# Seven products in another order, their token forms read beside the last gates, and the combined weights made beside linear attention

## The chip, the cores and the metric

The kernel runs on one core of one Trainium2 chip. The core has engines that run their own instruction queues in parallel: TensorE (PE, matmuls, with its weight loads shown as PEld), VectorE (DVE), ScalarE (ACT), GpSimd (POOL) and SyncE (SP), which here only issues DMAs. The metric is device microseconds for one execution; lower is better.

## The reference

One step of a hybrid decoder layer, in float32. 1024 prompt tokens with 16 learned meta tokens ahead of them, and 8 decode sequences of 4 tokens with a paged cache of 1024, go through one layer:

```python
h = rms_norm(x, norm_pre_g)
u = h @ w_in                      # q, k, v, gate of 8 stick-breaking heads; q, k, v, gate of 4 GLA heads
o_sb  = stick-breaking attention(q, k, v)        # prompt; decode: cached pages too
o_gla = gated linear attention(gq, gk, gv, log_f)  # state carried in chunks of 64
mixed = concat(o_sb * silu(sg), rms_norm(o_gla) * silu(gg))   # tokens x 2048
y = x + rms_norm(mixed @ w_out, norm_post_g)     # w_out: 2048 x 2048
```

The outputs are y for prompt and samples, the new keys and values, and the new GLA states.

## The kernel before

Each float32 matmul is made of three: both operands are split into a high and a low half of a shorter format (ACT casts the high half, DVE subtracts it for the low one), and PE adds high·high, high·low and low·high in PSUM (L289 to L291 for projections, L1410 to L1412 for the output).

The order of work in time is: load and norm; stick-breaking, eight heads with gates between (`head`); linear attention, four heads (`for g in range(GH)`, L905 and around), each with its projections gk, gq, gv; the cached values of decode with gates 5 to 13; gates 14 and 15; the output product; the last norm and stores. Each engine takes its instructions strictly in the order of its queue. The scheduler that makes the queues follows the program, and what `urgent()` marks is put ahead.

Side work is woven in by `W`, a counter of beats with a heap of generators. Each piece of PE work ends with `W.beat()`, which runs the generators that are due; a generator's `yield n` puts its next step n beats later, and `W.spawn(gen, delay)` starts it. A projection is 24 beats of six matmuls; a step of the output product is eight beats of twelve matmuls. The scores of the cached keys (L379 on DVE, with the loads `kp` and `qb` on SP) are woven in this way from stick-breaking to linear attention.

The output product `mixed @ w_out` for the 1024 prompt tokens is cut once in two along tokens, inner and outer dimension, and done with seven products of quarter size in place of eight. In the numbers of the code the token forms are:

- 1: a11; 2: a12; 4: a22, the quarters themselves, read from `md` in DRAM, where the gates store `mixed` transposed;
- 5: s1 = a21 + a22; 6: s2 = s1 − a11; 7: s3 = a21 − a11; 3: a12 − s2.

`form(p, gap)` (a generator) makes all eight tiles of a form: `combined` loads the quarters (128x512, 256 KB each) and adds or subtracts on DVE, and `split` makes the two halves (L1214 on ACT, then DVE). Form 6 also stores s1 and s2 to DRAM (`sd`), and forms 5 and 3 read them back (`stored`). The weight sides of products 5, 6, 7 and 4 are combined weights: `weight_forms` (L396 on) loads four quarters of w_out into one tile `tf` (`bufs=1`), does four subtracts on POOL (L405) and stores four results to `td` in DRAM, for 16 pairs of (k, q). It is spawned 120 beats into stick-breaking.

`weights` (L1270) loads a weight tile 128x512 (`wr`, three buffers), casts it (L1283, ACT) and makes the low half (L1284, DVE) in a ring of four. `step(p, q, banks, …)` runs eight k of product p for the column half q into four PSUM banks, and `take` then empties each bank: for p = 1 ACT copies it to `u` (L1321), for p = 2 DVE scales it and ACT squares it for the norm (L1325), and so on. The second product of a pair goes on adding in the same banks, so its first matmul waits until `take` has read them. The samples' 64 rows ride along as two more matmuls a k in products 1, 2, 7 and 3 (L1427, L1428). The order before is 1 2 (q = 0, then q = 1), 6 7, 5 3, then 4.

At the end `finish0` scales and adds the residual for token tiles 0 to 3 in 32 halves of 128x256 (L1377), each with its own load `xr`. The last step (4, 1) runs tile by tile from kept weights; after each of its four tiles `finish1` makes the norm (L162 to L168, L1365) and four scale-and-adds of 128x512 (L1404) for token tiles 4 to 7.

## Time and profile before

| what | value |
|---|---|
| three runs | 2226.03, 2229.82, 2230.07 us; median 2229.82 |
| the profiled execution | 2226.68 us, of which the span is 2225.0 |
| PE busy | 2109.9 us, 95% |
| DVE busy | 1667.0 us, 75% |
| ACT busy | 1001.5 us, 45% |
| POOL busy | 177.5 us, 8% |
| DMA moved | 317.15 MB, mean 143 GB/s |

Times in the profile are microseconds from the start of the span. In a row of the timeline stand the start, the duration, the engine, the line, the operation and its tiles (output, then inputs), and in brackets how long the engine stood idle before it and what ended that. In a row of the waits stand who waited, for whom, the total, how often, and the longest. In a row of groups stand the count, then busy time and mean ns of one, then the idle time just before them. A busy engine in a stretch is given in us of that stretch.

The stages lie in the span roughly so: stick-breaking with its gates 100 to 905, linear attention 905 to 1445 with gates to 1510, decode values with gates 5 to 13 up to 1790, gates 14 and 15 up to 1839, the output product 1839 to 2199, and 26 us behind the last matmul.

### The profile page before, as it was taken

The page shows a single profiled execution, that of the slowest core. Times are in us where ns is not written, and L with a number is a line of the kernel's source. Part 1 is how long each engine was busy: PE and PEld are TensorE (multiplying, and loading weights), DVE is VectorE, ACT ScalarE, POOL GpSimd, SP SyncE. Part 2 cuts the span into 40 slices and gives each one's busy share as a digit, 9 for nine tenths or more (in the row PEclk, how much of TensorE's full clock was granted, in tenths as well). Part 3 has the DMA queues.
Part 4 walks back from the last instruction along what each step waited for, and adds up shares of the span by engine and source line. Part 5 has one row for each costly group of instructions (what it writes and reads, how often), then busy time and mean ns, then how long its engine had stood idle before and what let it go on. Part 6 is the DMA issues. An engine that isn't in the chain of part 4 may idle for free. (4 is left out here: it accounts for less than half of the span.)

```text
span 2225.0 us, 43958 instructions
## 1 busy us (share of the span) xinstructions
PE 2109.9 (95%) x12640; PEld 1898.4 (85%) x12640; DVE 1667.0 (75%) x6712; ACT 1001.5 (45%) x2568; POOL 177.5 (8%) x364
## 2 busy tenths in 40 slices
PE   5999999999999999889999999999999998999995
PEld 4999999989998989888899998988777796677874
DVE  6367888878887789788888777778999945655457
ACT  7355556455554646324425342344443334433332
POOL 0001121211212021310000000000000000000000
PEclk9999999999999999999999999999999999999998
DMA  6224454444444455544443334345666637854367
GB/s 193 57 76 112 115 140 124 131 123 122 139 116 138 126 129 143 154 115 115 140 119 105 101 89 110 78 132 159 209 199 202 200 96 239 288 176 152 96 194 249
DMA packets 387428, 317.15 MB, mean 143 GB/s; under 512 B 50482, under 2 KB 324850, under 8 KB 386674
## 3 DMA queue, kind: packets, MB, share of 16 engines
q1 hardware_dynamic: 384994, 314.08, 49.2%
q8 instruction: 99, 1.62, 0.3%
q14 instruction: 143, 1.17, 0.2%
q10 hardware_dynamic: 2192, 0.27, 0.1%
HBM read 252.30 MB, written 61.92 MB: 141 GB/s over the span
## 5 line engine op out<-in xcount | busy, mean ns | idle before, releaser
L379 DVE SCALAR_TENSOR_TENSOR jk<-kp,qb 128x128 f32<-128x128 f32 x2048 | 512.8, 299 | 39.2 <-DMA kp<-in_cache_k_dram 33.5
L289 PE MATMUL acc_g<-hT,wh_g 128*128 128x368 f32 (+2 forms) x768 | 257.3, 335 | 0.2
L290 PE MATMUL acc_g<-hT,wh_g 128*128 128x368 f32 (+2 forms) x768 | 247.7, 323 | 0.0
L291 PE MATMUL acc_g<-hT,wl_g 128*128 128x368 f32 (+2 forms) x768 | 247.0, 322 | 0.0
L1410 PE MATMUL b<-ring,f 128*128 128x512 f32 x416 | 164.6, 397 | 9.7 <-ACT u L1321 5.1
L289 PEld LDWEIGHTS acc_g<-hT,wh_g 128*128 128x128 f32 x768 | 144.2, 188 | 33.1 <-issue 23.6
L379 DVE DVE_READ_ACCUMULATOR jk<-kp,qb 128x1 f32 x2048 | 164.2, 80 | 0.0
L1411 PE MATMUL b<-ring,f 128*128 128x512 f32 x416 | 163.9, 394 | 0.3 <-DVE ring L1284 0.3
L1412 PE MATMUL b<-ring,f 128*128 128x512 f32 x416 | 163.2, 393 | 0.0
L290 PEld LDWEIGHTS acc_g<-hT,wh_g 128*128 128x128 f32 x768 | 144.5, 188 | 1.0 <-issue 0.4
L291 PEld LDWEIGHTS acc_g<-hT,wl_g 128*128 128x128 f32 x768 | 144.3, 188 | 0.4 <-issue 0.4
L1284 DVE TENSOR_TENSOR ring<-wr,ring 128x512 fp32r<-128x512 f32 x104 | 71.4, 688 | 92.1 <-ACT ring L1283 91.5
L289 PE MATMUL acc_gv<-hT,wh_gv 128*128 128x384 f32 (+1 forms) x384 | 128.9, 336 | 4.5 <-ACT gq L959 4.5
L289 PE MATMUL acc_k<-hT,wh_k 128*128 128x378 f32 (+1 forms) x384 | 127.6, 332 | 0.0
L289 PE MATMUL acc_q<-hT,wh_q 128*128 128x368 f32 (+2 forms) x384 | 126.2, 329 | 0.0
L291 PE MATMUL acc_gv<-hT,wl_gv 128*128 128x384 f32 (+1 forms) x384 | 126.0, 328 | 0.0
L290 PE MATMUL acc_gv<-hT,wh_gv 128*128 128x384 f32 (+1 forms) x384 | 125.8, 328 | 0.0
L290 PE MATMUL acc_k<-hT,wh_k 128*128 128x378 f32 (+1 forms) x384 | 125.4, 326 | 0.0
L291 PE MATMUL acc_k<-hT,wl_k 128*128 128x378 f32 (+1 forms) x384 | 125.2, 326 | 0.0
L290 PE MATMUL acc_q<-hT,wh_q 128*128 128x368 f32 (+2 forms) x384 | 124.5, 324 | 0.0
L291 PE MATMUL acc_q<-hT,wl_q 128*128 128x368 f32 (+2 forms) x384 | 124.2, 324 | 0.0
L1283 ACT CAST ring<-wr 128x512 fp32r<-128x512 f32 x104 | 64.2, 619 | 126.2 <-PE sc L1427 56.8
(441 smaller groups left out, 5833.4 us busy)
## 6 DMA issues: line engine op xcount, KB each, us to landing
kp<-in_cache_k_dram SPq DMA_DIRECT2D x512, 64.0 KB
vr<-in_cache_v_dram SPq DMA_DIRECT2D x64, 512.0 KB
qb<-qsd SPq DMA_DIRECT2D x64, 256.0 KB
tf<-in_w_out_dram SPq DMA_DIRECT2D x64, 256.0 KB
td<-tf SPq DMA_DIRECT2D x64, 256.0 KB
wr_g<-in_w_in_dram SPq DMA_DIRECT2D x128, 128.0 KB
wr<-td SPq DMA_DIRECT2D x64, 256.0 KB
wr<-in_w_out_dram SPq DMA_DIRECT2D x48, 256.0 KB
```

The source lines that it names most:

```text
L289: mm(acc[c][:, :n], wh[:, k2, :], hh[k][:, lo:hi], start=(k == 0), stop=False)
L290: mm(acc[c][:, :n], wh[:, k2, :], hl[k][:, lo:hi], start=False, stop=False)
L291: W.mark = mm(acc[c][:, :n], wl[:, k2, :], hh[k][:, lo:hi], start=False, stop=(k == NK - 1)).ins
L379: ins = vec.scalar_tensor_tensor(jk[:], kp[:], 1.0, qbs[h, b][:, t, :], ALU.mult, ALU.mult, accum_out=zt[:, t, NPG - 1 - i:NPG - i])
L1283: act.copy(wh, r)
L1284: vec.tensor_tensor(wl, r, wh.bitcast(F32), ALU.subtract)
L1410: mm(bk[:], ah, wh, start=first and k == 0, stop=False, skip_group_check=True)
L1411: mm(bk[:], ah, wl, start=False, stop=False, skip_group_check=True)
L1412: mm(bk[:], al, wh, start=False, stop=last and k == 7, skip_group_check=True)
```

## The change

Three parts:

1. **Combined weights.** `weight_forms` is spawned 4 beats into linear attention, and no longer in stick-breaking. A pair (k, q) takes 26 beats in place of 44, and there is no pause behind the last store of a pair.
2. **Token forms.** Twenty-four tiles `a11`, `s3`, `s2` (eight each) come from a pool of 24 that is opened ahead of gate 14. `early` and `later` load 22 of the quarters beside gates 14 and 15 and make s3 = a21 − a11 and s2 = s3 + a22 on POOL; the last two of s2 follow in the first product. Forms 1, 6 and 7 are split from these tiles without a load; form 5 is a11 + s2, form 3 is a12 − s2, each with one load and one DVE step. `stored` and the stores to `sd` are gone. Later results (`u`, `y12`, `y22`) take over the 24 tiles.
3. **Order and end.** The products run as 1 2, 6, then 5 3, then 7 4, each pair for q = 0 and q = 1. `take` follows: after 5 the bank gives y22, after 3 y12, after 7 it is added to y22, after 4 to `u`. The sample rows ride on 1, 2, 3, 7. `finish0` starts after (3, 1) with 16 full tiles, and so do `load_keep` (the weights of (4, 1)) and `load_xr` (the residual of tiles 4 to 7). The last step goes on in the banks of (7, 1).

The core of the diff:

```diff
@@ weight_forms
                     spread(nc.sync.dma_start(t[:, i, :], w_out[0, r0:r0 + P, c0:c0 + 512]))
-                    yield 4
-                yield 4
+                    yield 3
+                yield 2
...
                 for j, i in enumerate((0, 2, 1, 3)):
-                    yield 4
+                    yield 2
                     spread(nc.sync.dma_start(td[j][:, k, q * 512:(q + 1) * 512], t[:, i, :]))
-                yield 4
...
-        W.spawn(weight_forms(), 120, lasting=True)
         for h in range(HEADS):
             head(h)
...
+        W.spawn(weight_forms(), 4)
         for g in range(GH):
...
-    gate_group(14)
-    load_small(0)
...
+        def early(k):
+            quarter(a11[k], 0, 0, k)
+            quarter(s3[k], 1, 0, k)
+            yield 2
+            pool.tensor_tensor(s3[k], s3[k], a11[k], ALU.subtract)
+
+        def later(k):
+            quarter(s2[k], 1, 1, k)
+            yield 2
+            pool.tensor_tensor(s2[k], s2[k], s3[k], ALU.add)
+
+        for k in range(8):
+            W.spawn(early(k), 2 + 2 * k)
+        for k in range(6):
+            W.spawn(later(k), 26 + 2 * k)
+        gate_group(14)
...
-            if p == 6:
-                x, y_, z = quarter(1, 0, k, p), quarter(1, 1, k, p), quarter(0, 0, k, p)
-                vec.tensor_tensor(x, x, y_, ALU.add)
-                nc.sync.dma_start(sd[0][k][:], x)
-                vec.tensor_tensor(z, x, z, ALU.subtract)
-                nc.sync.dma_start(sd[1][k][:], z)
-                return z
...
+            if p in (1, 6, 7):
+                return {1: a11, 6: s2, 7: s3}[p][k]
+            t = quarter(raw(f"q{p}_{k}")[:], p == 4, p in (2, 3, 4), k)
             if p == 5:
-                return stored(0, k)
...
+                vec.tensor_tensor(t, t, s2[k], ALU.add)
+            elif p == 3:
+                vec.tensor_tensor(t, t, s2[k], ALU.subtract)
+            return t
...
-                    for f in range(2):
-                        fs = slice(f * 256, (f + 1) * 256)
-                        x = stage(f"xr{i}_{b}_{f}")[:, :256]
-                        nc.sync.dma_start(x, x_prompt[0, i * P:(i + 1) * P, b * 512 + f * 256:b * 512 + (f + 1) * 256])
-                        vec.scalar_tensor_tensor(o[:, fs], o[:, fs], r[:, i:i + 1], x, ALU.mult, ALU.add)
...
+                    x = raw(f"xr{i}_{b}")[:]
+                    nc.sync.dma_start(x, x_prompt[0, i * P:(i + 1) * P, cs])
+                    vec.scalar_tensor_tensor(o, o, r[:, i:i + 1], x, ALU.mult, ALU.add)
...
-        AFTER = {(1, 1): lambda: W.spawn(form(7, 2)), (2, 1): lambda: W.spawn(form(5, 4)), (6, 1): lambda: W.spawn(form(3, 2)),
-                 (7, 1): lambda: W.spawn(form(4, 4))}
-        for pa, pb in ((1, 2), (6, 7), (5, 3)):
...
+        AFTER = {(1, 1): lambda: W.spawn(form(5, 2)), (2, 1): lambda: W.spawn(form(3, 2), 8), (6, 1): lambda: W.spawn(form(7, 2)),
+                 (5, 1): lambda: W.spawn(form(4, 2)),
+                 (3, 1): lambda: (W.spawn(finish0()), W.spawn(load_keep(), 4), W.spawn(load_xr(), 17))}
+        for pair in ((1, 2), (6,), (5, 3), (7, 4)):
```

What the queues become, at three places. First SP at the start of the output product. In the rows of before, `wr` is a weight tile, `go`, `md` belong to gate 15, and `qFalseFalse` are the quarters of form 1; behind "waits" stand the queues and engines that a row waits for:

```order
L1282 DMA wr_0_31394<-in_w_out_dram 128x512 [waits DMAHW2_49,DMAHW3_49,DVE_49,DMAHW5_49,PE_49,Pool_49]
L1282 DMA wr_1_31419<-in_w_out_dram 128x512
L1282 DMA wr_2_31443<-in_w_out_dram 128x512 [waits DMAHW4_49]
L418 DMA go_768_31296<-od_108 128x304 [waits DVE_49]
L428 DMA md_124<-gs_16_31260 128x368 [waits DVE_49]
L1223 DMA qFalseFalse_1_31321<-md_109 128x512 [waits DMAHW7_49]
L1282 DMA wr_3_31468<-in_w_out_dram 128x512 [waits DMAHW2_49,DMAHW0_49,DVE_49]
```

The same place in the rows after; `s_6` is a quarter of s2, `q_0` and `q_1` are quarters of form 2:

```order
L1198 DMA s_6_30855<-md_123 128x512 [waits DMAHW6_49,DMAHW2_49]
L417 DMA go_16_31321<-od_108 128x368 [waits DMAHW7_49]
L417 DMA go_384_31340<-od_108 128x384 [waits DMAHW0_49]
L1294 DMA wr_0_31439<-in_w_out_dram 128x512 [waits DMAHW1_49,DMAHW3_49,DVE_49,PE_49]
L1294 DMA wr_1_31466<-in_w_out_dram 128x512
L1294 DMA wr_2_31490<-in_w_out_dram 128x512
L1198 DMA q_0_31460<-md_117 128x512
L417 DMA go_768_31359<-od_108 128x304 [waits DVE_49]
L1198 DMA q_1_31484<-md_118 128x512 [waits DMAHW6_49]
```

The loads of form 1 are gone from here, the first weight load waits for PE as it did, and loads of form 2 have moved up behind it.

Second, DVE's last rows. Before, `b` is a bank, `u`, `y`, `c` are results, and L1377 are finish0's halves:

```order
L1365 TENSOR_REDUCE tot_34131<-yssq 128x1
L1345 TENSOR_TENSOR u_3_31984<-b_3_34151,u_3_31984 128x512
L162 TENSOR_SCALAR v_y_34085<-tot_34083 128x1
L1377 SCALAR_TENSOR_TENSOR y_1_3_32719<-y_1_3_32719,r_y_33691,xr_3_0_34025 128x256
L1347 TENSOR_TENSOR u_3_31984<-u_3_31984,gpost_105_33658 128x512
L1377 SCALAR_TENSOR_TENSOR y_1_3_32719<-y_1_3_32719,r_y_33691,xr_3_1_34028 128x256
L165 TENSOR_TENSOR t_y_34135<-r_y_34134 128x1
```

After, from the last tile's add on:

```order
L1360 TENSOR_TENSOR u_3_31990<-b_3_33656,u_3_31990 128x512
L168 TENSOR_TENSOR r_y_34032<-r_y_34032,t_y_34033 128x1
L1426 SCALAR_TENSOR_TENSOR u_2_31643<-u_2_31643,r_y_34032,xrs_33677 128x512
L1426 SCALAR_TENSOR_TENSOR u_2_31988<-u_2_31988,r_y_34032,xrs_33678 128x512
L1426 SCALAR_TENSOR_TENSOR y_0_2_32691<-y_0_2_32691,r_y_34032,xr_2_2_33907 128x512
L1426 SCALAR_TENSOR_TENSOR y_1_2_33012<-y_1_2_33012,r_y_34032,xr_2_3_33912 128x512
L1331 TENSOR_TENSOR u_3_31990<-u_3_31990,gpost_115_33859 128x512
L1379 TENSOR_REDUCE tot_34076<-yssq 128x1
```

No step of finish0 stands there any more; the four scale-and-adds of tile 2 stand between the add of tile 3 and its small steps.

Third, SP in linear attention, after: `tf` is the tile of combined weights, `td` their stores, `kp` a page of cached keys, `wr_gv` the projection's weights.

```order
L409 DMA td_130<-tf_0_15960 128x512 [waits DMAHW3_49,Pool_49]
L180 DMA wr_gv_0_0_16881<-in_w_in_dram 128x2x128 [waits DMAHW4_49,DVE_49]
L330 TENSOR_LOAD pt
L330 ISA x2
L337 ISA
L337 DMA kp_4_5_16554<-in_cache_k_dram 128x128 [waits DMAHW5_49]
L401 DMA tf_1_16540<-in_w_out_dram 128x512 [waits DMAHW6_49,DMAHW3_49,DMAHW1_49]
```

The next tile's first load comes a few rows behind the last store of the tile before and waits on DMA queues; the projection's weights and the pages share SP. Before, four of the sixteen `tf` tiles come in linear attention; now all sixteen do.

More of the change, by code (lines that the diff above doesn't have):

```diff
@@ L1188, in load_small, with ytile, quarter @@
             nc.sync.dma_start(small[c][:, k, :], md[8 * c + k][:, SEQ:TOUT])
-    gate_group(14)
-    load_small(0)
-    vec.tensor_tensor(small[0][:], small[0][:], osmp[:], ALU.mult)
-    gate_group(15)
-    wp_cm.__exit__(None, None, None)
-    with tc.tile_pool(name="op", bufs=2) as op, tc.tile_pool(name="ops", bufs=1, space=PSUM) as ops:
+    with ExitStack() as out:
+        oy = out.enter_context(tc.tile_pool(name="oy", bufs=24))
+        def ytile(nm):
+            return oy.tile([P, 512], F32, tag="y", name=nm)[:]
+        def quarter(dst, r, c, k):
+            nc.sync.dma_start(dst, md[8 * c + k][:, 512 * r:512 * r + 512])
+            return dst
+        a11, s3, s2 = [[ytile(f"{nm}_{k}") for k in range(8)] for nm in ("a11", "s3", "s2")]
+        def early(k):
[12 more added lines that the diff above has]
+        gate_group(14)
+        load_small(0)
+        vec.tensor_tensor(small[0][:], small[0][:], osmp[:], ALU.mult)
+        gate_group(15)
+        wp_cm.__exit__(None, None, None)
+        op = out.enter_context(tc.tile_pool(name="op", bufs=2))
+        ops = out.enter_context(tc.tile_pool(name="ops", bufs=1, space=PSUM))
         rep = op.tile([P, 4, NSMP], F32, tag="rep", bufs=1, name="rep")
@@ L1291, in hybrid_step @@
         load_small(1)
+        for k in range(6, 8):
+            W.spawn(later(k))
         W.spawn(form(2, 1))
-        W.spawn(form(6, 3), 10)
+        W.spawn(form(6, 2), 10)
         ysm = [op.tile([P, 256], F32, tag=f"ysm{f}", bufs=1, name=f"ysm{f}") for f in range(2)]
         sssm = op.tile([P, 2], F32, tag="sssm", bufs=1, name="sssm")
-        ssq = op.tile([P, 8, 6], F32, tag="yssq", bufs=1, name="yssq")
+        ssq = op.tile([P, 8, 8], F32, tag="yssq", bufs=1, name="yssq")
         pool.memset(ssq[:], 0.0)
@@ L1431, in step @@
                 take(p, q, t, banks[t])
-            if p in (2, 3):
+            if p in (2, 7):
                 sample_y(SB[c, q], 2 * c + q)
-        def need(b):
-            gains[b] = gain(b)
-        AFTER = {(1, 1): lambda: W.spawn(form(7, 2)), (2, 1): lambda: W.spawn(form(5, 4)), (6, 1): lambda: W.spawn(form(3, 2)),
-                 (7, 1): lambda: W.spawn(form(4, 4))}
-        for pa, pb in ((1, 2), (6, 7), (5, 3)):
-            for q in range(2):
-                if pa != 6:
-                    need(q if pa == 1 else 2 + q)
-                banks = [bank(f"b{pa}{q}_{t}") for t in range(4)]
-                for p in (pa, pb):
-                    step(p, q, banks, p == pa, p == pb)
-                    AFTER.get((p, q), lambda: None)()
@@ L1448, in hybrid_step @@
-        W.spawn(finish0())
-        W.spawn(finish_samples())
-        for q in range(2):
-            need(q)
-        xr = []
-        for i in range(4):
-            xr.append(slot(REGION["C"][i], f"xr{i}")[:, :D].bitcast(F32))
-            nc.sync.dma_start(xr[i], x_prompt[0, 512 + i * P:512 + (i + 1) * P])
-        step(4, 0, [bank(f"b40_{t}") for t in range(4)], True, True)
-        keep = [slot(REGION["B"][i], f"keep{i}") for i in range(4)]
-        kept = [weights(4, 1, k, [keep[k // 2][:, (2 * (k % 2) + i) * 512:(2 * (k % 2) + i + 1) * 512] for i in range(2)])
-                for k in range(8)]
+        xr, keep = {}, []
@@ new lines, in load_keep @@
+        def load_keep():
+            keep.extend(slot(REGION["B"][i], f"keep{i}") for i in range(4))
+            for k in range(8):
+                kept.append(weights(4, 1, k, [keep[k // 2][:, (2 * (k % 2) + i) * 512:(2 * (k % 2) + i + 1) * 512] for i in range(2)]))
+                yield 2
+        kept = []
+        AFTER = {(1, 1): lambda: W.spawn(form(5, 2)), (2, 1): lambda: W.spawn(form(3, 2), 8), (6, 1): lambda: W.spawn(form(7, 2)),
+                 (5, 1): lambda: W.spawn(form(4, 2)),
+                 (3, 1): lambda: (W.spawn(finish0()), W.spawn(load_keep(), 4), W.spawn(load_xr(), 17))}
@@ new lines, in hybrid_step @@
+        for pair in ((1, 2), (6,), (5, 3), (7, 4)):
+            for q in range(2):
+                banks = [bank(f"b{pair[0]}{q}_{t}") for t in range(4)]
+                for p in pair:
+                    b = {2: q, 3: 2 + q, 7: 2 + q, 4: q}.get(p)
+                    if b is not None:
+                        gains[b] = gain(b)
+                    if (p, q) != (4, 1):
+                        step(p, q, banks, p == pair[0], p == pair[-1])
+                        AFTER.get((p, q), lambda: None)()
@@ L1461, in hybrid_step @@
+        W.spawn(finish_samples())
         for t in range(4):
-            bk = bank(f"b41_{t}")
             for k in range(8):
-                product(bk, t, 4, k, kept[k], True, True)
+                product(banks[t], t, 4, k, kept[k], False, True)
                 W.beat()
-            take(4, 1, t, bk)
+            take(4, 1, t, banks[t])
             finish1(t)
```

72 lines of the change are left out of this document (33 added, 39 removed).

## The prediction

> **What bounds the kernel now.** I read the windows view by stage first: columns are the stretch, its length, busy time of PE, PEld, DVE, ACT, POOL, the granted PE clock, the DMA share and GB/s. The rows are stick-breaking (200 to 905), linear attention (905 to 1445), decode (1445 to 1790), gates 14 and 15, the first products, and the end after the last matmul.
>
> ```profile
> span 2225.0 us, 43958 instructions
> 200.00:905.00 705.00, 684.79 (x4112) 646.53 (x4111) 571.86 (x2791) 388.14 (x980) 125.85 (x245) 1.00 0.48 129
> 905.00:1445.00 540.00, 516.34 (x3313) 485.84 (x3312) 432.31 (x2289) 204.24 (x587) 34.00 (x51) 0.99 0.42 112
> 1445.00:1790.00 345.00, 338.46 (x2368) 282.58 (x2366) 306.00 (x718) 141.11 (x346) 6.56 (x23) 1.00 0.60 181
> 1790.00:1839.00 49.00, 49.00 (x315) 48.14 (x314) 18.61 (x56) 18.87 (x57) 0.00 (x0) 1.00 0.31 86
> 1839.00:1965.00 126.00, 112.33 (x460) 83.87 (x459) 77.31 (x138) 56.64 (x120) 0.29 (x1) 0.96 0.83 267
> 2199.00:2225.00 26.00, 0.01 (x1) 0.00 (x0) 17.54 (x46) 2.55 (x10) 0.00 (x0) 0.58 0.81 283
> ```
>
> PE is the bound nearly everywhere, and the change removes no matmul. So only PE's idle time can be won or lost: 20.2 us in stick-breaking, 23.7 in linear attention, 13.7 at the start of the products, 26.0 at the end. Next, PE's longest wait in the products (total, times, longest), and PE's timeline at three places where it stood (in brackets the idle time before, and what ended it):
>
> ```profile
> PE b L1410 <- ACT u L1321: 5.1, 3, 3.0
> ...
> 1843.28 0.69 PE L1427 MATMUL sc<-ring,f 128*64 128x512 f32 x1 [4.03 <-ACT ring L1283]
> 1848.85 0.40 PE L1410 MATMUL b<-ring,f 128*128 128x512 f32 x1
> ...
> 1875.73 0.80 PE L1410 MATMUL b<-ring,f 128*128 128x512 f32 x1 [2.97 <-ACT u L1321]
> 1878.88 0.39 PE L1411 MATMUL b<-ring,f 128*128 128x512 f32 x1
> 1879.11 0.39 PE L1412 MATMUL b<-ring,f 128*128 128x512 f32 x1
> ...
> 1964.54 0.79 PE L1410 MATMUL b<-ring,f 128*128 128x512 f32 x1 [0.48 <-ACT b L1325]
> 1967.66 0.40 PE L1411 MATMUL b<-ring,f 128*128 128x512 f32 x1
> ```
>
> At speed a matmul starts every 0.23 us (1878.88 to 1879.11). After each of the three stops one starts every 0.45 us: seven in 1875.73 to 1878.88, 3.15 us where 1.6 would do; seven in 1964.54 to 1967.66, the same; twelve in 1843.28 to 1848.85, 5.57 for 2.8. So slow matmuls add 1.5, 1.5 and 2.8 us to the 13.7 idle: the start of the products loses 19.5 us. The Trainium skill, page TensorE: Matmul & The Clock Gate (Part 1), says the clock falls only after about 3.4 us without work. By that rule the 2.97 us stop would cost no slow matmuls and the term would be 1.5 smaller; here the row shows them, and the row decides.
>
> **The products' start.** The transfers of 1840 to 1960, from the DMA view:
>
> ```profile
> q1 hardware_dynamic: 18049, 32.28, 83.7%
> q<-md SPq DMA_DIRECT2D x42, 256.0 KB
> sd<-q SPq DMA_DIRECT2D x16, 256.0 KB
> ...
> 1839.32 1.28 SPq L1282 DMA_DIRECT2D wr<-in_w_out_dram  x3
> ...
> 1842.61 0.62 ACT L1283 CAST ring<-wr 128x512 fp32r<-128x512 f32 x1 [0.16 <-DMA wr<-in_w_out_dram]
> ...
> 1873.42 1.25 ACT L1214 CAST f<-qFalseTrue 128x512 fp32r<-128x512 f32 x2 [1.12 <-DMA qFalseTrue<-md]
> 1961.82 0.62 ACT L1283 CAST ring<-wr 128x512 fp32r<-128x512 f32 x1 [4.44 <-DMA wr<-td]
> ```
>
> PE's stops are banks that ACT empties late (L1321 copies product 1's bank, L1325 squares product 2's). ACT works in order, and ahead of them in its queue stands a cast whose source is still in flight: at 1873.42 product 2's token form, at 1961.82 a weight tile that ACT had waited 4.44 us for, while the DMA engines are 84% busy with the loads and stores above and the weights. Now product 1's and 6's forms come from tiles that POOL fills beside the gates; in this stretch only products 2 and 5 load quarters, 16 of them, and s2 two late ones. That takes away about 40 of these 58 transfers, 10 of the 32 MB. So I count the later stops as gone: 19.5 less the first (4.0 idle, 2.8 slow) and 0.5 of small waits is 12.2 us. The first stays: SP issues the first weight load at 1839.32, since it waits for the room of the gates' weights, and ACT casts it at 1842.61, as soon as it lands; in the new order (SP's rows in the section on the change) that load still waits for PE there. Bounds: 0, if ACT is late for another reason, and 19.5.
>
> **The late products.** finish0's 16 loads and 16 stores, now full tiles, move from the end into (7,0), (4,0), (7,1), where load_xr and load_keep run too. With 32 weight tiles, some 8 tiles of xr, 4 gains and 4 quarters it is 80 transfers of 0.262 MB, 21 MB. The three steps hold 320 matmuls, 73 us at 0.23: 288 GB/s. The stretch lies between these two cases: the first products' row above (267 GB/s, 13.7 us idle) and the last products of before:
>
> ```profile
> 2140.00:2199.00 59.00, 58.48 (x257) 46.91 (x255) 40.38 (x92) 19.53 (x47) 0.00 (x0) 1.00 0.71 227
> ```
>
> At 227 GB/s PE lost 0.5 us. SP is one queue in order, so weight loads now stand behind finish0's stores, which wait for DVE. I take 3 us lost, bounds 0 and 13.7; 3 rather than the middle since few token forms are due there, so ACT's casts wait for weights alone. The number of banks that one product must empty before the next writes them is the same, six switches. Net for the products: −9 (−19 to +6).
>
> **The end.** Groups of the last 26 us, then DVE's last row:
>
> ```profile
> L1404 DVE SCALAR_TENSOR_TENSOR u<-u,r_y,xr 128x512 f32<-128x512 f32 x6 | 4.3, 749 | 0.1
> L1377 DVE SCALAR_TENSOR_TENSOR y<-y,r_y,xr 128x256 f32<-128x256 f32 x8 | 3.7, 481 | 2.0 <-DMA xr<-in_x_prompt_dram 2.0
> L1345 DVE TENSOR_TENSOR u<-b,u 128x512 f32<-128x512 f32 x2 | 1.4, 684 | 0.0
> L1346 ACT ACTIVATE b<-u 128x512 f32<-128x512 f32 x2 | 1.2, 601 | 9.3 <-DVE u L1345 9.3
> L164 ACT ACTIVATE r_y<-r_y 128x1 f32<-128x1 f32 x3 | 0.6, 203 | 0.1
> ...
> 2217.50 1.41 DVE L1404 SCALAR_TENSOR_TENSOR y<-y,r_y,xr 128x512 f32<-128x512 f32 x2
> ```
>
> DVE's queue holds finish0's halves (L1377, waiting for their xr) in between, and that is what delays the last tiles: with finish0 gone, the path after the last matmul is an add of 0.68, a square of 0.60, nine small steps like L164 (0.20 each at most: 1.8) and four scale-and-adds of 0.75, overlapping to 1.41 a pair (2.8): 5.9 us. From DVE's last instruction (2217.50 + 1.41 = 2218.91) to the end of the span are 6.1 for the last stores. Together 12.0. The new order puts tile 2's four scale-and-adds ahead of tile 3's small steps: 2.8 more, 14.8; I take 15. So −11. Bounds: 12 (−14), and 21 (−5) if half of finish0's 16 full tiles (8 × 0.75 = 6 us) slips into the end.
>
> **The combined weights.** Their 64 subtracts go from stick-breaking to linear attention. POOL's groups of before in the two stages, then two places of the timeline, and the wait of PE on the split's low half:
>
> ```profile
> L405 POOL TENSOR_TENSOR tf<-tf 128x512 f32<-128x512 f32 x48 | 68.8, 1433 | 9.5 <-DMA tf<-in_w_out_dram 7.7
> ...
> L405 POOL TENSOR_TENSOR tf<-tf 128x512 f32<-128x512 f32 x16 | 22.6, 1412 | 160.2 <-DMA tf<-in_w_out_dram 120.3 <-DMA kp<-in_cache_k_dram 39.4
> ...
> 480.51 1.37 POOL L405 TENSOR_TENSOR tf<-tf 128x512 f32<-128x512 f32 x1
> 480.65 1.38 DVE L379 SCALAR_TENSOR_TENSOR jk<-kp,qb 128x128 f32<-128x128 f32 x1
> 481.96 0.28 DVE L379 SCALAR_TENSOR_TENSOR jk<-kp,qb 128x128 f32<-128x128 f32 x1
> ...
> 712.30 2.85 POOL L405 TENSOR_TENSOR tf<-tf 128x512 f32<-128x512 f32 x2
> 713.95 1.38 DVE L488 TENSOR_TENSOR lo_s<-X,hi_s 127x158 fp32r<-127x158 f32 x1
> 715.38 0.34 PE L524 MATMUL z<-lo_s,ntri 127*127 127x158 f32 x1 [1.97 <-DVE lo_s L488]
> ...
> PE z L524 <- DVE lo_s L488: 9.8, 11, 2.3
> ```
>
> A DVE instruction beside a subtract takes 1.38 us where the same one takes 0.28, 1.1 more, and at 715.38 PE waits 1.97 for it. So 16 subtracts are in linear attention already and 48 move. What they cost PE in stick-breaking is at most its idle time, 20.2/48 = 0.42 us each, at least nothing; I take the 9.8 of the wait on lo_s, 0.2 each. In linear attention the two halves of before, with the 16 subtracts and without, say:
>
> ```profile
> 938.00:1127.00 189.00, 175.68 (x1116) 164.24 (x1116) 157.66 (x794) 64.77 (x189) 27.24 (x25) 0.99 0.46 125
> 1127.00:1445.00 318.00, 313.29 (x2043) 295.24 (x2043) 253.83 (x1386) 127.26 (x368) 0.00 (x0) 0.99 0.38 99
> ```
>
> Idle 13.3 us in 189 with them; without them 4.7 in 318, which is 2.8 per 189: 10.5 over 16, at most 0.66 each, since the first group's start is in the same stretch. At least 0. I take 0.25, a little above stick-breaking's 0.2: DVE is as full in both (81% and 80%), but the subtracts will stand closer. So −10 (−20 to 0) there and +12 (0 to +32) here. Each tile's four loads and four stores move with it, 96 transfers or 25 MB: 47 GB/s on top of 112, less than decode's 181. On SP a tile's first load now stands a few rows behind the last store of the tile before, in the same buffer; it waits until the stores have landed, and linear attention's weight and key loads are queued behind it. The 16 subtracts of before had their transfers there too, so that price is inside the 0 to 0.66. The Trainium skill, page SBUF — State Buffer (Who interferes with whom), states that a VectorE instruction with two SBUF inputs and a GpSimd one that reads SBUF exclude each other for a whole instruction. The 1.38 beside 1.37 agrees. By that page each subtract may hold DVE for its full 1.4, and DVE may hold POOL's new steps beside the gates as well.
>
> **Gates 14 and 15** get 22 loads (5.8 MB, 118 GB/s more in 49 us, where 86 stood) and 14 POOL steps; SP puts two or three loads before each weight load. PE had no idle time and DVE 18.6 of 49: +1 (0 to +3); with the cover gone it would be one late weight load, like the 2.97 above. The rest I cost at nothing: the two combining steps of products 6 and 7 leave DVE (77 of 126 busy) for POOL, idle then; new homes of forms and wider sums of squares change no count on PE.
>
> **Sum.** −9 −11 −10 +12 +1 = −17 on the profiled execution, 2226.68 (1.68 around its span): 2209.7. The three runs were 2226.03 to 2230.07, median 2229.82; I set **2210** as median.
>
> **Rivals.**
>
> (a) Slower: DVE in linear attention becomes the bound. 48 more subtracts of 1.1 us put 53 us on DVE's 432 of 540 (90%). Decode ran DVE at 306 of 345 (89%) with PE losing 6.5 only, which speaks against; the 13.3 idle in 189 speaks for it. It decides from 0.25 + (17 + 4.5)/48 = 0.7 us of PE a subtract: 48 × 0.7 = 34 in place of 12 gives 2232. Chance 0.12. By the whole 1.4 of the Trainium skill's page SBUF — State Buffer it would be 67 us on DVE, 92%, the same case a little nearer.
>
> (b) The late products choke: SP's stores ahead of weights make a stop like 1875.73 (2.97 + 1.5) in three steps, 13 in place of 3, and 6 us slip into the end: 2226, about no change; half of it 2218. Against it: 2140 to 2199 ran 227 GB/s with 0.5 lost. Chance 0.16.
>
> (c) It all goes well: stick-breaking gives 20, linear attention takes 5, the products 15: 2210 − 10 − 7 − 6 = 2187. Against it: nothing shows that linear attention's 0.66 is all due to the first group. Chance 0.1.
>
> (d) The early forms don't do what they say, since the stops come from ACT and the weights and not the forms: the products' −9 becomes +3, 2222. Chance 0.07. The forecast has 0.55.
>
> The range, 2188 to 2231, leaves out most of (c) and the worse half of (a). A measurement here can tell about 0.2% (4.5 us) from no change: faster is the forecast, (c), (d) and the better half of (b), 0.80; within it 0.08; slower 0.12.
>
> **What would show it.** Right: idle at 1843 as before and none over 1 us at the next switches; after the last matmul about 15 us; idle in stick-breaking down to 10; in linear attention up by 12, with DVE's L379 and X steps long beside L405. Wrong: linear attention longer by over 30, or PE waiting for ring (L1294's cast) in products 7 and 4.

## The result and the profile after

The changed kernel took 2244.78 us (median of 8 runs, 2239.08 to 2253.59), the kernel before 2228.28 (8 runs, 2225.07 to 2230.07). The ratio is 1.0082, with a 95% interval from 1.0063 to 1.0101: slower by 0.8%, where 2210 was forecast. The profiled execution of the changed kernel took 2243.48 us, its span is 2241.8, 16.8 longer than before.

PE executes the same 12,640 matmuls, so both spans can be cut at the same places of its stream. The rows of the changed kernel's PE timeline at the cuts (the first matmul of linear attention, of gate 3, of gate 14, the last of gate 15 with the first product's behind it, and the last of all):

```profile
880.83 0.33 PE L289 MATMUL acc_gk<-hT,wh_gk 128*128 128x384 f32 x1
...
1445.46 0.41 PE L289 MATMUL acc_g<-hT,wh_g 128*128 128x368 f32 x1
...
1819.56 0.44 PE L289 MATMUL acc_g<-hT,wh_g 128*128 128x368 f32 x1
...
1867.89 0.30 PE L291 MATMUL acc_g<-hT,wl_g 128*128 128x304 f32 x1
1873.24 1.22 PE L1432 MATMUL b<-ring,f 128*128 128x512 f32 x2 [5.04 <-ACT ring L1295]
...
2228.96 0.39 PE L1434 MATMUL b<-keep,f 128*128 128x512 f32 x1
```

And of before:

```profile
907.59 0.33 PE L289 MATMUL acc_gk<-hT,wh_gk 128*128 128x384 f32 x1
...
1437.27 0.41 PE L289 MATMUL acc_g<-hT,wh_g 128*128 128x368 f32 x1
...
1792.18 0.43 PE L289 MATMUL acc_g<-hT,wh_g 128*128 128x368 f32 x1
...
2198.62 0.39 PE L1412 MATMUL b<-keep,f 128*128 128x512 f32 x1
```

The lengths between the cuts, with gate 15 of before ending at 1839.2, beside what the prediction's terms said (each stage is read from the one profiled execution):

| stage | before | after | difference | predicted |
|---|---|---|---|---|
| up to linear attention (stick-breaking) | 907.6 | 880.8 | −26.8 | −10 |
| linear attention | 529.7 | 564.6 | +34.9 | +12 |
| gates 3 to 13 with decode | 354.9 | 374.1 | +19.2 | 0 |
| gates 14 and 15 | 47.1 | 48.6 | +1.6 | +1 |
| products | 359.8 | 361.2 | +1.4 | −9 |
| behind the last matmul | 26.0 | 12.4 | −13.5 | −11 |
| sum | 2225.0 | 2241.8 | +16.8 | −17 |

**Linear attention.** PE's longest wait in it after (total, times, longest):

```profile
PE P_d L754 <- DVE at L750: 14.8, 4, 7.4
```

The same wait before:

```profile
PE P_d L756 <- DVE at L752: 0.3, 1, 0.3
```

The timeline after, ahead of that wait's longest stop, POOL, DVE, then PE:

```profile
938.43 2.78 POOL L405 TENSOR_TENSOR tf<-tf 128x512 f32<-128x512 f32 x2 [2.05 <-DMA tf<-in_w_out_dram]
...
938.48 1.39 DVE L379 SCALAR_TENSOR_TENSOR jk<-kp,qb 128x128 f32<-128x128 f32 x1
940.02 1.48 DVE L185 TENSOR_TENSOR wl_gv<-wr_gv,wh_gv 128x256 fp32r<-128x256 f32 x1
942.85 0.29 DVE L379 SCALAR_TENSOR_TENSOR jk<-kp,qb 128x128 f32<-128x128 f32 x1 [1.35 <-DMA kp<-in_cache_k_dram]
...
949.93 0.40 PE L754 MATMUL P_d<-gq,gk 128*48 128x48 f32 x2 [7.39 <-DVE at L750]
```

And the groups of the key scores on DVE and of the subtracts on POOL (count, then busy time and mean ns, then idle time before them), with the key scores of before in the last row:

```profile
L379 DVE SCALAR_TENSOR_TENSOR jk<-kp,qb 128x128 f32<-128x128 f32 x769 | 212.3, 326 | 29.9 <-DMA kp<-in_cache_k_dram 28.2 <-issue 1.1
L405 POOL TENSOR_TENSOR tf<-tf 128x512 f32<-128x512 f32 x60 | 85.5, 1425 | 449.3 <-DMA tf<-in_w_out_dram 201.2 <-DMA kp<-in_cache_k_dram 158.5 <-DMA Sb<-in_state_gla_dram 35.6
L379 DVE SCALAR_TENSOR_TENSOR jk<-kp,qb 128x128 f32<-128x128 f32 x776 | 187.0, 291 | 13.4 <-DMA kp<-in_cache_k_dram 10.4 <-issue 1.8 <-DVE jk L379 0.6
```

Sixty of the 64 subtracts fall into this stage, the last four into decode. Two in a row (938.43) run from 938.43 to 941.21, and the two DVE instructions beside them take 1.39 and 1.48 us; the same ones just before take 0.28 and 0.41. The key scores (L379) take 326 ns on average where they took 291, and DVE stands 28.2 us for key pages where it stood 10.4. Which of the two PE pays for can't be read here; the runs below tell. In stick-breaking, the wait on lo_s that was 9.8 us is gone but for this row:

```profile
PE z L523 <- DVE lo_s L487: 0.6, 1, 0.6
```

**Decode.** PE has hardly more idle time there (8.5 us where 6.5 stood), but the matmuls dO of the values run otherwise. Each uses 32 columns of the array, and four on four column groups start together. Before, eight of one step:

```profile
1558.38 0.41 PE L1070 MATMUL dO<-vr,dA 128*32 128x512 bf16 x2
1558.38 0.40 PE L1070 MATMUL dO<-vvr,dA 128*32 128x512 bf16 x1
1558.39 0.61 PE L1070 MATMUL dO<-vv,dA 128*32 128x512 bf16 x2
1558.62 0.39 PE L1070 MATMUL dO<-vr,dA 128*32 128x512 bf16 x2
1558.63 0.39 PE L1070 MATMUL dO<-vvr,dA 128*32 128x512 bf16 x1
1558.95 0.43 PE L289 MATMUL acc_g<-hT,wh_g 128*128 128x368 f32 x1
```

The eight take 0.57 us, up to the gate's next matmul. After, the first step's come in smaller runs between the gate's matmuls:

```profile
1553.60 0.60 PE L1069 MATMUL dO<-vn,an 128*32 128x512 bf16 x2
...
1556.77 0.62 PE L1069 MATMUL dO<-vr,dA 128*32 128x512 bf16 x2
1557.32 0.43 PE L289 MATMUL acc_g<-hT,wh_g 128*128 128x368 f32 x1
```

Two take 0.55 us, as long as eight did. In PE's queue the 576 of them stand in 64 runs of eight or sixteen before, and in 83 after, many of two to six in the first samples. The diff doesn't touch this code; the scheduler orders it by when it reckons each operand ready.

**Products.** PE's waits after:

```profile
PE b L1432 <- ACT ring L1295: 5.0, 1, 5.0
PE b L1432 <- ACT b L1330: 4.3, 1, 4.3
PE b L1432 <- ACT u L1339: 3.4, 1, 3.4
PE b L1432 <- DVE y L1357: 2.8, 1, 2.8
```

What DVE, SP and ACT stood at, in their timelines:

```profile
1899.97 0.69 DVE L1255 TENSOR_TENSOR q<-q,s 128x512 f32<-128x512 f32 x1 [5.66 <-DMA q<-md]
1900.58 0.69 DVE L1296 TENSOR_TENSOR ring<-wr,ring 128x512 fp32r<-128x512 f32 x1
1901.29 6.71 SPq L1294 DMA_DIRECT2D wr<-in_w_out_dram  x4
1904.33 0.62 ACT L1295 CAST ring<-wr 128x512 fp32r<-128x512 f32 x1 [4.96 <-DMA wr<-in_w_out_dram]
...
2148.71 0.75 DVE L1390 SCALAR_TENSOR_TENSOR c<-c,r_y,xr 128x512 f32<-128x512 f32 x1 [1.23 <-DMA xr<-in_x_prompt_dram]
...
2178.61 1.14 ACT L1295 CAST ring<-wr 128x512 fp32r<-128x512 f32 x2 [4.26 <-DMA wr<-td]
2179.65 0.59 ACT L1330 ACTIVATE b<-u 128x512 f32<-128x512 f32 x1
```

Of the stops of before only the first (5.0, was 4.0) and the one from (1, 0) to (2, 0) (3.4, was 3.0) are left. Two new ones stand at the switches from (7, 0) to (4, 0) (2.8) and from (4, 0) to (7, 1) (4.3). Ahead of the stop at (2, 0), DVE's queue holds a step of form 5 (L1255), a product that comes some 120 us later, in front of the ring's low halves (L1296), and stands 5.66 us for its load. The low half at 1900.58 comes behind it; only when that is done does SP load the next weight tile into the buffer (1901.29), and ACT, whose copy of the bank stands behind the cast of that tile, waits 4.96 us. Ahead of the last stop, ACT's square (L1330), which frees the bank, stands behind two weight casts, the first of which waits 4.26 us.

**The end.** DVE's last pair ends at 2236.93 + 1.41 = 2238.34, 3.4 us ahead of the span's end, where 6.1 us lay before:

```profile
2236.93 1.41 DVE L1426 SCALAR_TENSOR_TENSOR y<-y,r_y,xr 128x512 f32<-128x512 f32 x2
```

### The profile page after: what moved, and what is told of

The parts are those of the page before. It is cut to its first block, busy times and chain, and to the rows that moved or that the text cites. A ratio compares the mean times of both kernels' runs of the same rounds, so it can differ in the third digit from the quotient of the medians.

```text
span 2241.8 us, 43812 instructions
## 1 busy us (share of the span) xinstructions
PE 2129.0 (95%) x12640; PEld 1913.8 (85%) x12640; DVE 1665.4 (74%) x6680; ACT 999.7 (45%) x2568; POOL 200.5 (9%) x380
## 5 line engine op out<-in xcount | busy, mean ns | idle before, releaser
L379 DVE SCALAR_TENSOR_TENSOR jk<-kp,qb 128x128 f32<-128x128 f32 x2048 | 518.9, 303 | 65.1 <-DMA kp<-in_cache_k_dram 60.8
L289 PEld LDWEIGHTS acc_g<-hT,wh_g 128*128 128x128 f32 x768 | 145.4, 189 | 35.9 <-issue 22.9
L379 DVE DVE_READ_ACCUMULATOR jk<-kp,qb 128x1 f32 x2048 | 167.6, 82 | 0.0
L1296 DVE TENSOR_TENSOR ring<-wr,ring 128x512 fp32r<-128x512 f32 x104 | 71.2, 690 | 120.5 <-ACT ring L1295 120.2
L405 POOL TENSOR_TENSOR tf<-tf 128x512 f32<-128x512 f32 x64 | 90.6, 1416 | 484.0 <-DMA tf<-in_w_out_dram 206.8
```

The source lines that it names most:

```text
L289: mm(acc[c][:, :n], wh[:, k2, :], hh[k][:, lo:hi], start=(k == 0), stop=False)
L379: ins = vec.scalar_tensor_tensor(jk[:], kp[:], 1.0, qbs[h, b][:, t, :], ALU.mult, ALU.mult, accum_out=zt[:, t, NPG - 1 - i:NPG - i])
L405: spread(pool.tensor_tensor(t[:, i, :], t[:, a, :], t[:, b, :], ALU.subtract))
L1296: vec.tensor_tensor(wl, r, wh.bitcast(F32), ALU.subtract)
```

## The experiments

The theory: (1) a subtract on POOL costs PE some 0.55 to 0.6 us through DVE, in either stage, so the move wins in one what it loses in the other; (2) the transfers beside linear attention cost the rest there, and by way of the scheduler's reckoning break the runs of dO; (3) the late products take back what the early ones win. The rivals stand with each run. Each run lists its median beside runs of the kernel before on the same chip, and its stages in the table at the end of this section.

### The move

**Combined weights back in stick-breaking**, with the beats of before (44 for a tile), the rest as changed:

```diff
+        W.spawn(weight_forms(), 120, lasting=True)
         for h in range(HEADS):
...
-        W.spawn(weight_forms(), 4)
         for g in range(GH):
```

> The changed kernel with its combined weights made in stick-breaking again, as before; token forms, product order and end stay as changed. In PE's queue the decode matmuls dO stand in 64 runs of eight or sixteen again, where the changed kernel has 83 runs, many of two to six. If moving the combined weights costs +8 us (stick-breaking -27, linear attention +35) and, through that order, most of the +19 of the decode stage: 2244.8 - 8 - 17 = 2220 us, and the decode stage back at 355 us. Rival, that the decode stage is longer for another reason (the new tiles, later transfers): 2237, decode stage still 370 or more.

2219.24 us, ratio 0.9971 (0.9957 to 0.9984). Decode is back at 355.8. Without the move the other two parts make the kernel 0.3% faster.

**The move alone**, in the kernel before (the same edit the other way round):

> The kernel before with its combined weights made beside linear attention, and nothing else changed. PE's queue has the 83 runs of dO of the changed kernel. If this part alone is what made the change slower: 2228.3 + 8 + 17 = 2253 us, with stick-breaking 27 us shorter, linear attention 35 longer, decode 17 longer, and the products and the end as before. Rival, that the parts hurt each other (token forms need the DMA and DVE that the combined weights take): 2236, with decode not over 5 us longer.

2256.56 us, ratio 1.0138 (1.0117 to 1.0158). The stages moved by −27.5, +36.1, +19.7: the loss belongs to this part alone.

**No subtracts**, transfers and beats kept:

```diff
-                    spread(pool.tensor_tensor(t[:, i, :], t[:, a, :], t[:, b, :], ALU.subtract))
```

> The changed kernel without the 64 subtracts of the combined weights on POOL; loads, stores and their beats stay, so products 5, 6, 7 and 4 take unsubtracted weights. PE's queue keeps the 83 runs of dO. If the subtracts hold DVE and that is what PE pays: linear attention falls from 565 us to 525 to 535, and the whole to about 2208, with decode still 17 us longer than before. Rival, that the transfers on SP's queue delay key pages and weights: linear attention stays over 555, the whole over 2235.

2206.09 us, ratio 0.9913 (0.9892 to 0.9934). Linear attention falls to 529.1: 35.5 us less over its 60 subtracts, 0.59 each. DVE still stands for the key pages, even longer, as the first row says, from its waits in linear attention. PE's wait on P_d stays too (second row), and ahead of its longest stop DVE stands for a page (third row, from DVE's timeline):

```profile
DVE jk L379 <- DMA kp<-in_cache_k_dram: 34.3, 29, 4.1
PE P_d L753 <- DVE at L749: 10.8, 3, 6.8
...
940.85 0.29 DVE L379 SCALAR_TENSOR_TENSOR jk<-kp,qb 128x128 f32<-128x128 f32 x1 [4.06 <-DMA kp<-in_cache_k_dram]
```

So the late pages are not what the 35.5 us paid for. They cost PE as well, in the wait on P_d, where 10.8 of 14.8 us stay when no subtract runs. Decode stays 16 longer, with the 83 runs: the transfers and their beats break the runs, not the subtracts.

**dO's four in reverse**, in the changed kernel:

```diff
-            for j, (p0, v) in enumerate(((0, 0), (2, 0), (0, 1), (0, 2))):
+            for j, (p0, v) in reversed(list(enumerate(((0, 0), (2, 0), (0, 1), (0, 2))))):
```

> The changed kernel with the four column-group matmuls of a value product issued in reverse, the one whose operand is ready last first; 68 runs of dO in PE's queue, nearly all of eight or sixteen, in place of 83. If the broken runs cost the decode stage its time: 12 to 17 us less, 2229 us, decode stage near 358 us. Rival, that values and weights arrive late there: 2245, decode stage still 374.

2235.92 us, ratio 1.0050 (1.0030 to 1.0070), against 1.0082. Decode falls by 12.5, to 361.6. The profiled execution as a whole is only 4.4 us shorter, since stick-breaking (+4.2) and linear attention (+5.1), which the edit doesn't touch, came out longer in it; the medians lie 9 apart. The runs carry 12.5 of the 19.2 us, in one execution of each.

### The engine

**Subtracts in pieces**, on the first experiment's kernel:

```diff
-                    spread(pool.tensor_tensor(t[:, i, :], t[:, a, :], t[:, b, :], ALU.subtract))
-                    yield 1
+                    for cs in (slice(x, x + P) for x in range(0, 512, P)):
+                        spread(pool.tensor_tensor(t[:, i, cs], t[:, a, cs], t[:, b, cs], ALU.subtract))
+                        yield 1
```

> The changed kernel with its combined weights made in stick-breaking (as in the first experiment, 2219.2 us), each subtract cut into four pieces of 128x128 with a beat behind each; the same beats for a tile in all. If POOL holds a two-input DVE instruction for the length of one POOL instruction, a piece of some 0.35 us holds it 0.3 us in place of 1.1, mostly inside the slack that DVE has: stick-breaking up to linear attention 885 to 895 us in place of 910, the whole 2199 to 2209. Rival, that what counts is POOL's total time beside DVE, however cut: 910 or more, 2219 or more.

2212.44 us, ratio 0.9938 (0.9917 to 0.9958); 894.7 up to linear attention, 15.4 less. POOL's group in stick-breaking:

```profile
L406 POOL TENSOR_TENSOR tf<-tf 128x128 f32<-128x128 f32 x192 | 101.0, 552 | 6.1 <-DMA tf<-in_w_out_dram 6.0
```

POOL is busy longer, 101.0 us in place of 68.8, and PE loses less. DVE loses no less: up to linear attention it is busy as long as with whole subtracts. The first row is that of the first experiment, the second this run's; behind the length stand the busy times of PE, PEld and DVE:

```profile
0.00:910.10 910.10, 867.15 (x5192) 818.56 (x5193) 687.79 (x3227) 502.15 (x1272) 135.96 (x289) 0.99 0.45 124
0.00:894.70 894.70, 863.21 (x5192) 814.75 (x5193) 685.98 (x3237) 501.59 (x1272) 167.23 (x433) 1.00 0.46 126
```

So neither POOL's total time nor DVE's sets the price, but how the holds fall. The edit makes the single hold shorter and also spreads the holds over more beats; it doesn't tell the one from the other. In linear attention the pieces of the other 16 subtracts gained nothing (532.4 beside 529.7), which stays open. The whole came 3 us above the range; in its profile the products are 3.4 and linear attention 2.7 longer than in the first experiment.

**Subtracts on DVE**, on the first experiment's kernel:

```diff
-                    spread(pool.tensor_tensor(t[:, i, :], t[:, a, :], t[:, b, :], ALU.subtract))
+                    spread(vec.tensor_tensor(t[:, i, :], t[:, a, :], t[:, b, :], ALU.subtract))
```

> The changed kernel with its combined weights made in stick-breaking (2219.2 us), and the 64 subtracts on DVE itself in place of POOL. A 128x512 step takes DVE 0.69 us, where a POOL one held it 1.1. If the price is the time that DVE loses, it falls to about 0.6 of 27 us: 2208, linear attention reached at 899. Rival, that DVE's queue in order makes it worse, since the subtract now waits for its loads with everything else behind it: 2225 or more.

2188.62 us, ratio 0.9826 (0.9796 to 0.9856): 30.6 us less, where 11 were expected. The tile's view says why it is cheap:

```profile
L405 DVE TENSOR_TENSOR tf<-tf x64: 672/682/693, 241.1 to 1108.5; 128x512 f32<-128x512 f32 x64
```

0.68 us each, 0.69 at most. The same view of the kernel before:

```profile
L405 POOL TENSOR_TENSOR tf<-tf x64: 1250/1326/3267, 239.2 to 1124.7; 128x512 f32<-128x512 f32 x64
```

The columns are least, median and longest ns. My expectation scaled PE's price with the time that DVE loses; the price doesn't scale. That a step of 0.68 fits into DVE's slack, and holds of 1.1 close together don't, is the reading that fits; no run measures the slack.

**The same one line in the kernel before**:

> The kernel before with nothing changed but the 64 subtracts on DVE in place of POOL. If POOL beside DVE costs PE 0.5 us for each subtract wherever it stands: stick-breaking 23 us shorter, linear attention 9 us shorter, the whole 2195. Rival, that the gain on DVE needed the changed products: 2220 or more.

2198.17 us, ratio 0.9888 (0.9861 to 0.9915). Stick-breaking is 22.3 shorter, linear attention 10.0.

**The same one line in the changed kernel**:

> The changed kernel (2244.8 us) with nothing else changed but the 64 subtracts on DVE in place of POOL; they stay beside linear attention, and PE's queue keeps the 83 runs of dO. If the engine makes the price and not the place: linear attention 530 to 540 us in place of 565, decode 370 to 374 as it was, the whole 2213 to 2220. Rival, that DVE is too full beside linear attention whoever subtracts: over 555, the whole over 2235.

2205.49 us, ratio 0.9912 (0.9888 to 0.9935), 7.5 us below the range. Linear attention takes 532.8 with its subtracts (58 here) on DVE, 3.7 more than with none. So the engine makes the price, not the place. What is left of the move, beside the version with the weights in stick-breaking and the subtracts on DVE: 6.7 us won up to linear attention, 12.4 lost in it, 10.6 lost in decode (368.5).

### The late products

All of these stand on the first experiment's kernel, from the third on with the subtracts on DVE.

**finish0's xr two steps ahead** (its 16 loads issued two steps before the steps that read them):

> The changed kernel with its combined weights made in stick-breaking (2219.2 us), and finish0 loading its xr tiles two steps ahead of the step on DVE that reads them. If DVE's queue standing at finish0's wait for xr makes the stops at the switches from product 7 to 4 (2.8 and 1.3 us, with slow matmuls behind them some 7): both under 0.5 us, products 5 to 7 us shorter, 2213. Rival, that weights come late there because the DMA engines and SP are full: the stops stay, 2219.

2219.01 us, ratio 0.9968 (0.9950 to 0.9985), products 360.0: no effect, the stops stay (1.8 and 3.2 us). DVE's wait for xr in products 7 and 4 did not shrink with the edit but grew, from 1.0 to 4.6 us, so this run tells neither for the wait nor for the rival; the run without the loads, below, does.

**Quarter loads held** until their beat:

```diff
-            t = quarter(raw(f"q{p}_{k}")[:], p == 4, p in (2, 3, 4), k)
+            t = raw(f"q{p}_{k}")[:]
+            spread(nc.sync.dma_start(t, md[8 * (p in (2, 3, 4)) + k][:, 512 * (p == 4):512 * (p == 4) + 512]))
...
-            mm(bk[:], al, wh, start=False, stop=last and k == 7, skip_group_check=True)
+            W.mark = mm(bk[:], al, wh, start=False, stop=last and k == 7, skip_group_check=True).ins
```

> The changed kernel with its combined weights made in stick-breaking (2219.2 us), and the quarter loads of forms 2, 5, 3 and 4 held behind the matmul of their due beat, so that form 5's five loads and DVE steps no longer stand in the first product's queues. If these make the stop at the switch from product 1 to 2 (3.8 us and 1.5 of slow matmuls): under 1 us, products 4 to 5 us shorter, 2214.5. Rival, that form 2's own loads or the first weights make it: 2219.

2213.19 us, ratio 0.9946 (0.9926 to 0.9967), products 353.8, 4.6 less; the stop is 1.6 us where 3.8 stood. Early quarter loads made most of it. All forms are held here; the one whose step stands in front in the changed kernel's row (1899.97) is form 5.

**All late loads held too** (the loads of `finish0`, `load_keep` and `load_xr` with `spread` as well):

> The changed kernel with its combined weights in stick-breaking, subtracted on DVE (2188.6 us), the quarter loads held behind the matmul of their due beat (5 us less, as shown), and held in the same way the loads of finish0, of load_keep and of load_xr. If the stops at the switches from product 7 to 4 come from these loads standing ahead of the ring's weights on SP: 6 us less again, products 348 to 351 us, the whole 2178. Rival, that the stops come from the sum of the transfers there: products 356 to 360, the whole 2184.

2211.34 us, ratio 0.9940 (0.9919 to 0.9961): 25 us more than with the quarter loads alone held (2185.91, the next run), products 384.1. I had it the wrong way round. SP's timeline in products 7 and 4:

```profile
2083.71 0.42 SPq L1393 DMA_DIRECT2D xr<-in_x_prompt_dram  x1
2084.22 1.35 SPq L1296 DMA_DIRECT2D wr<-td  x3
2087.96 0.34 SPq L1395 DMA_DIRECT2D out_dram<-c  x1
2088.35 0.42 SPq L1393 DMA_DIRECT2D xr<-in_x_prompt_dram  x1
...
2092.59 0.34 SPq L1395 DMA_DIRECT2D out_dram<-c  x1
```

It turns in a circle: a store waits for finish0's step on DVE, that for its xr, which was issued just behind the store before; the next store goes out 4.25 us after that load (2083.71 to 2087.96), and weights go only in between. DVE stands 21.6 us for xr here and 2.6 where only the quarters are held, and PE 21.5 us for weights. Held loads make the circle; where they are not held, the scheduler issues some of them ahead of the stores.

**Quarter loads held, subtracts on DVE**:

> The version that the runs so far point to: the changed kernel, combined weights in stick-breaking, their subtracts on DVE (2188.6 us), the quarter loads of the forms held behind the matmul of their due beat (5 us less, as shown), and finish0, load_keep and load_xr as the change has them. If both gains add: 2184 us, products 357 to 359. Rival, that holding moves the forms into a later crowd, as holding the late loads did: 2188 or more.

2185.91 us, ratio 0.9824 (0.9804 to 0.9844); its profile 2181.6 of span, products 355.4 where 363.3 stood. The whole lies between what was expected and the rival, and its ratio can't be told from the 0.9826 without the hold.

**Without finish0's xr loads**:

```diff
-                    x = raw(f"xr{i}_{b}")[:]
-                    nc.sync.dma_start(x, x_prompt[0, i * P:(i + 1) * P, cs])
-                    vec.scalar_tensor_tensor(o, o, r[:, i:i + 1], x, ALU.mult, ALU.add)
+                    vec.scalar_tensor_tensor(o, o, r[:, i:i + 1], o, ALU.mult, ALU.add)
```

> The same version with finish0's 16 loads of xr left out (its step on DVE reads the result itself in place of xr, so the residual is missing in token tiles 0 to 3); the steps on DVE and the 16 stores stay. If DVE's and SP's queues waiting for xr make the stops at the switches from 7 to 4: these under 0.5 us each, products 350 to 353 us, 6 us less than the version with the loads. Rival, that the stores, which wait for DVE and stand ahead of weights on SP, or load_keep in the same three buffers make them: products 356 to 359.

2184.14 us, ratio 0.9819 (0.9801 to 0.9837), products 356.4, stops of 1.8 and 3.5: the loads of xr are not it.

**Product 4's squares off the bank**:

```diff
-                done(u, 4 + t, q, [bk[:]])
+                done(u, 4 + t, q, [stage(f"jk4{q}_{t}_{f}")[:, :256] for f in range(2)])
```

> The best version so far (2185.9 us) with the squares behind product 4 writing their junk to a stage tile, as those behind product 7 do, so that a bank is free for the next product after DVE's add and no longer after ACT's square. If ACT's square, standing behind two weight casts in ACT's queue, makes the stop of 3.8 us at the switch from (4, 0) to (7, 1): that stop under 0.5 us, products 350 to 351 us, the whole 2181. Rival, that the weights themselves are late there: PE stops for the ring in its place, products 354 to 356.

2182.13 us, ratio 0.9813 (0.9791 to 0.9835), products 354.1. The whole came out as expected and the stop did not, so the number is luck: the stop at (7, 1) is 2.7 where 3.8 stood, and now waits for DVE, as PE's waits say:

```profile
PE b L1434 <- DVE u L1362: 2.7, 1, 2.7
```

**load_keep through other buffers** (`tag="fr", bufs=5` for its tiles in `weights`):

> The best version so far (2185.9 us) with load_keep's weights loaded through the five buffers of the token forms' raw tiles in place of the ring's three. If load_keep in the ring's buffers is what makes the ring's weights late and so ACT's casts: the stop of 3.8 us goes to under 1, products 350 to 352 us. Rival: 354 to 356.

2187.03 us, ratio 0.9827 (0.9803 to 0.9850), products 353.4 in the profile; the stop at 7 to 4 is gone, the one at (7, 1) is 2.7. Against its base (0.9824) neither this nor the run before is a difference that can be told, and the last stop was anything from 1.3 to 4.3 us in the versions without these two edits. What makes it stays open.

The stages in the profiled executions, us:

| kernel | to lin. att. | lin. att. | decode | g 14, 15 | products | end |
|---|---|---|---|---|---|---|
| before | 907.6 | 529.7 | 354.9 | 47.1 | 359.8 | 26.0 |
| after | 880.8 | 564.6 | 374.1 | 48.6 | 361.2 | 12.4 |
| weights back | 910.1 | 529.7 | 355.8 | 49.9 | 358.3 | 12.4 |
| move alone | 880.1 | 565.8 | 374.6 | 47.7 | 358.5 | 24.0 |
| no subtracts | 882.6 | 529.1 | 370.9 | 48.9 | 358.0 | 12.4 |
| dO in reverse | 885.0 | 569.7 | 361.6 | 50.3 | 358.5 | 12.5 |
| pieces | 894.7 | 532.4 | 357.5 | 49.3 | 361.7 | 12.4 |
| xr ahead | 907.4 | 530.5 | 356.1 | 49.0 | 360.0 | 12.4 |
| quarters held | 909.0 | 530.5 | 356.1 | 49.5 | 353.8 | 12.4 |
| subtracts on DVE | 887.2 | 520.4 | 357.9 | 49.8 | 363.3 | 12.6 |
| before, on DVE | 885.3 | 519.7 | 358.3 | 47.4 | 360.6 | 25.2 |
| after, on DVE | 880.5 | 532.8 | 368.5 | 49.3 | 363.3 | 12.6 |
| DVE, quarters held | 885.9 | 521.9 | 356.5 | 49.3 | 355.4 | 12.6 |
| all late loads held | 885.9 | 518.1 | 358.3 | 49.6 | 384.1 | 12.6 |
| no xr loads | 886.0 | 519.9 | 355.3 | 48.8 | 356.4 | 12.5 |
| squares off the bank | 883.9 | 522.3 | 358.0 | 48.9 | 354.1 | 13.1 |
| keep in other buffers | 886.3 | 520.0 | 356.7 | 49.0 | 353.4 | 13.1 |

Each row is one execution. Between versions that treat a stage alike it differs by 3 to 5 us: up to linear attention 907.4 to 910.1 with whole subtracts on POOL and 883.9 to 887.2 with them on DVE, decode 354.9 to 358.3 with 64 runs of dO, the changed products 358.0 to 363.3 with no load held and 353.4 to 356.4 with the quarter loads held. The gains by engine and by runs of dO stand clear of that, the one by held quarters just so; a difference of 3 us in one stage doesn't.

## Why the prediction was wrong

**The steps that failed.** The sum was 33.8 us too low: linear attention took 22.9 more than its term, decode 19.2 and the products 10.4, while stick-breaking won 16.8 more than its term and the end 2.5 (gates 14 and 15: 0.6). The price of the subtracts was put at less than half of what it is in both stages, but the two terms that rest on it miss by only 6.1 us together; the largest error that nothing makes up for is decode, a term put at nothing without a reason.

**The price of the subtracts.** The prediction took 0.2 us each from one named wait (on lo_s, 9.8 us) in stick-breaking, and 0.25 in linear attention. The runs give 26.8/48 = 0.56 in the one, transfers included, and 0.59 in the other. The bound for stick-breaking, all its idle time (0.42), was itself too low: up to linear attention PE's idle time fell by 20.6 us, from 44.7 to 24.1, and the same matmuls were busy 6.2 us less. The slow matmuls behind each stop count as busy; the prediction had reckoned them for the products and not here. With about one price for both places the move is nothing won: −26.8 there, +25.5 of the 35.5 here (the 16 that stood here before cost 10.0, by the run on DVE). The rest of linear attention's 34.9, 9.4 us, stays when the subtracts go: 529.1 with the transfers and no subtract, against 519.7 with a quarter of them and 16 subtracts on DVE. The wait on P_d, 10.8 us without a subtract and 0.3 before, is where it shows. The prediction priced that at part of the 0.25.

**What it left out** is decode, +19.2. No term, rival or bound gave it more time, though PE's order could be read ahead of the run: the change moved PE's queue at a place that the diff doesn't touch. The runs of dO account for 12.5. The other 6.7 were not taken apart: with 83 runs the stage took 374.1 and 374.6 with the subtracts on POOL, 370.9 with none and 368.5 with them on DVE.

**The products**: the term was −12.2 and +3, measured +1.4. The early stops went as forecast, except the one at the first switch, which the scheduler rebuilt: the steps of form 5 in DVE's queue hold up the weights, and ACT with them (holding all quarter loads took 4.6 us off the products). The new stops in products 7 and 4, 2.8 and 4.3 us with slow matmuls behind, stand where rival (b) put them. Its mechanism, weights late behind finish0's stores, is not shown: leaving out xr's loads changed nothing, and the stores alone were not tried.

**Right**: the start stayed (5.0 for 4.0), as the row of SP's first weight load said; gates 14 and 15 cost 1.6 for 1; the end won 13.5 for 11, since the last stores took 3.4 us behind DVE's last step and not 6.1. DVE's path in front of them was right: 9.0 us for 8.7.

Rival (a), slower through DVE in linear attention, forecast +34 for that stage, and 34.9 came; the sign "longer by over 30" held too. Its mechanism did not: DVE did not become the bound. It was busy 461.3 of 564.6 us (82%) with the subtracts on POOL and 447.2 of 532.8 (84%) with them on DVE itself, where they cost 3.7 us. What PE pays for is single holds, long or close together, and of the 34.9 some 9.4 came another way, so the match is in part luck; its 2232 missed, since it left stick-breaking and decode as they were forecast.

The Trainium skill's page SBUF — State Buffer (Who interferes with whom) says that a VectorE instruction with two SBUF inputs and a GpSimd one that reads SBUF shut each other out for a whole instruction; the 1.39 and 1.48 us agree, and so does the gain from shorter pieces in stick-breaking.

The parts that work make a kernel that beats both: token forms, order and end as changed, the weights in stick-breaking, subtracted on DVE, quarters held, squares off the bank: 2182.13 us, ratio to before 0.9813 (0.9791 to 0.9835).

## What to carry to other kernels

Before work is moved away from where it hurts, measure what it costs per instruction in the place it goes to; here that was the same, and giving it to the engine that it was meant to relieve took 28 to 39 us off three versions by one word. When a scheduler makes the queues, compare the whole order of every engine, and most of all where the diff changes nothing: the matmuls that share the array cost 12.5 us when they were no longer neighbours. A price read from one wait's row was too low here, by more than half; cutting both spans at the same instructions gives the whole.

## What the runs showed of the hardware

- A helper engine can cost more than the help: a 128x512 subtract on POOL takes 1.25 to 3.27 us and makes a DVE instruction beside it 1.1 us longer (1.38 for 0.28); the same step on DVE takes 0.68, and 30.6 us less of the whole. Cut in four, with DVE busy as long (686.0 and 687.8 us), it cost PE 15.4 us less.
- Two dO matmuls alone took 0.55 us of PE between the gate's matmuls, eight together 0.57.
- A PE stop costs more than its length: up to linear attention the changed kernel won 26.8 us, of which 20.6 were idle time of PE and 6.2 busy time of the same matmuls.
